# Where the summed weights of the feed-forward are kept: an SBUF tile or a PSUM bank

## The chip, the cores and the metric

The kernel runs on one core of a Trainium2 chip. Its metric is the device time of one launch in microseconds (us). A core has a matrix engine (PE, with its weight loads shown as PEld), a vector engine (DVE), a scalar engine (ACT), a general engine (POOL) and a queue engine (SP) that here issues nearly all DMAs. Each engine works through its own list of instructions in order; waits between engines are semaphores. SBUF is the on-chip working memory; PSUM, eight banks of 128 partitions by 512 fp32 values, is where PE puts its results. [...]

## The reference, cut to what matters

Two transformer layers on 512 tokens of width 1024, the first one also on 256 context tokens. Each layer ends in a gated feed-forward with 2816 hidden values, and only that part is touched:

```python
def swiglu(h, w_in, w_out):
    g, u = jnp.split(h @ w_in, 2, axis=-1)
    return (jax.nn.silu(g) * u) @ w_out
...
h = h + g2 * swiglu(modulate(h, norm2_g[l], sh2, sc2), ffn_w_in[l], ffn_w_out[l])
```

In the first layer (`l` = 0) the context tokens go through the same weights, so the feed-forward works on 768 columns there and on 512 in the second layer (`l` = 1).

## The kernel before

**The tiling.** `ffn(l)` walks over 22 inner pairs `f`. A pair is the 128 hidden values of the gate and the 128 of the up branch with the same number; its weights come in one DMA of 1024 KB, the tile `raw` of 128 x 2048 (`ffn_in`, line 792). Cut in four blocks of 128 x 512 it is `a11`, `a12` (gate, first and second half of the model width) and `a21`, `a22` (up). The tokens are cut in halves too, so the pair is a product of 2 x 2 blocks, which the kernel makes with seven block products in place of eight (Strassen's scheme in Winograd's form). The products are numbered 1 to 7 and made in the order 2, 1, 5, 6, 3, 7, 4.

**The weights of a product.** `weights(n, f, plain)` (line 915) supplies what product `n` multiplies by. Products 1, 2 and 4 take a block of `raw` as it is. Products 5, 6, 3 and 7 take a sum, made by DVE on line 925 in one tile `t` that is written anew each time:

| product | line 925 makes | tensors read |
|---|---|---|
| 5 | t = a21 + a22 | two blocks of raw |
| 6 | t = t - a11 | t and a block of raw |
| 3 | t = a12 - t | a block of raw and t |
| 7 | t = a11 - a21 | two blocks of raw |

Each block is then split into a high and a low part of the type fp32r by `slot` (line 898): ACT copies the block into the high half of a ring tile `w` (line 901), and a subtraction, block minus high part, writes the low half (line 903). That subtraction runs on DVE for the sums of pairs `f` > 2 and on POOL for everything else. The next version of `t` can be written only when the copy and the subtraction have both read the last one. The ring holds 6 slots in the first layer and 10 in the second. `mm3` multiplies the parts with three matmuls (lines 99 to 101): high by high, high by low, low by high.

**Where `t` lies.** Line 918 picks the tile once for each pair. Pairs with `f % 3 == 2` use the tile of the sums of squares (`sumsq()`, one buffer, shown as `sq` in the profile), the others use `tmp("t")`, which has two buffers. So three SBUF buffers go round by pairs. The `raw` tiles go round in the same three places, so `raw` of pair `f` + 3 is loaded when the last reader of `raw` of pair `f` is through.

**PSUM.** `fill()` (line 48) is a tag with one bank, `bank()` one with three, `wide()` one with two double banks: eight in all. In the feed-forward `fill` holds the second product of the pairs 0, 1 and 2 (line 942), and from pair 3 on product 2 goes to a `bank()`; `fill` isn't used again until the end of the feed-forward.

**The order of the work.** The pairs 0 to 2 are worked together, product by product. From pair 3 on each pair's seven products stand between parts of the second matmul of the feed-forward (`s2`, its result added into `xT` and `ctxT` on line 757). In the first layer the list is also filled up with dot products for the next layer's modulation (`junk`, line 220, DVE). The kernel's text gives priorities; a planner that simulates the engines then lays down the order of each engine's list, and an instruction is placed where the planner has its inputs and its tile ready.

DVE reads the results of the products out of PSUM: line 964 after product 1, 975 after 3, 979 after 7, 984 after 4. Products 1, 6, 7 and 4 add up in the same bank, so PE can start 4 only when line 979 has read what 7 left.

Of the kernel before, what the change touches and what calls it, by code (L numbers as in the profile page):

```python
# [26 lines left out]
class Builder:  # L27
# [814 lines left out]
    def ffn(self, l):  # L842
# [53 lines left out]
        raws, sums, state = {}, {}, {}  # L896

        def slot(src, t=None, eng=None):
            t = ring.tile([P, 2, 512], F32R, name=self.uid("w"), tag="w", bufs=(6, 10)[l]) if t is None else t
            with tc.issue_after(self.first_sq.ins) if self.nslot < 12 else ExitStack():  # L900
                nc.scalar.copy(t[:, 0, :], src)  # L901
            self.nslot += 1
            (eng or nc.gpsimd).tensor_tensor(t[:, 1, :], src, t[:, 0, :].bitcast(F32), ALU.subtract)  # L903
            return t
# [10 lines left out]
        def weights(n, f, plain):  # L915
            if f not in raws:
                raws[f] = self.raws.pop(f) if f < 2 else self.ffn_in(l, f, ring if f % 3 == 2 else self.Rf)
                sums[f] = self.sumsq()[:, :512] if f % 3 == 2 else self.tmp("t")
            r, t = raws[f], sums[f]
            a11, a12, a21, a22 = [r[:, i * 512:(i + 1) * 512] for i in range(4)]  # L920
            for v, x, y, how in ((5, a21, a22, ALU.add), (6, t, a11, ALU.subtract), (3, a12, t, ALU.subtract),
                                 (7, a11, a21, ALU.subtract)):
                if v == n:
                    with tc.issue_after(self.last_diag.ins) if both and f < 3 and n == 5 else ExitStack():
                        nc.vector.tensor_tensor(t, x, y, how)  # L925
            if plain:
                return {1: a11, 2: a12}[n]
            return slot({1: a11, 2: a12, 4: a22}[n]) if n in (1, 2, 4) else slot(t, eng=nc.vector if f > 2 else None)
# [7 lines left out]
        def product(n, f):  # L936

            plain = n in (1, 2) and f in self.plain
            w = weights(n, f, plain)
            st = state.setdefault(f, {})  # L940
            if n == 2:
# [401 lines left out]
```

## Time and profile before

| | |
|---|---|
| median of 3 runs | 1676.35 us (1673.29 to 1677.78) |
| the profiled execution | 1676.23 us, of which 1674.4 us is the span from its first to its last instruction |
| mean granted PE clock | 0.971 of full speed |
| ACT busy | 729.3 us, 44% of the span |
| POOL busy | 658.4 us, 39% |
| line 903 on POOL, low parts of plain blocks of raw | 126 x 1391 ns |
| line 901 on ACT, high parts of `t` | 120 x 621 ns |

The page gives for each engine its busy time and the number of its instructions, and then groups of instructions by source line: busy time, mean duration of one, and the idle time of the engine just before them with what ended it. A group's tile names drop their numbers, so `t` stands for every buffer of that tag. Other views give the waits between engines, the chain of work that ended last, a list of instructions in order of time, and busy times by stretch of time. The feed-forward of the first layer runs from about 410 to 960 us, that of the second from about 1255 to 1650 us.

### The profile page before, as it was taken

How to read it: one execution, taken by the hardware profiler on the slowest of the kernel's cores; microseconds unless marked ns; L12 is line 12 of the kernel's file. 1: busy time of each engine (PE TensorE's matmuls, PEld its weight loads, DVE VectorE, ACT ScalarE, POOL GpSimd, SP SyncE). 2: the span in 40 equal slices, each digit the busy share in tenths (PEclk: the TensorE clock that was granted, in tenths of full speed). 3: DMA queues.
4: the chain of work that ended last, by engine and by line, in shares of the span. 5: the costliest groups of instructions: out<-in, count | busy, mean ns of one | idle time of the engine just before them, and what ended most of it. 6: DMA issues, size and time to landing. Idle time of an engine off the chain costs nothing.

```text
span 1674.4 us, 24582 instructions
## 1 busy us (share of the span) xinstructions
PE 1550.9 (93%) x9463; PEld 1358.2 (81%) x9463; DVE 1152.9 (69%) x2097; ACT 729.3 (44%) x1464; POOL 658.4 (39%) x477
## 2 busy tenths in 40 slices
PE   6999989799889899999999988999986899999996
PEld 4776878699689899999999877767776788888886
DVE  4622788855987889777766675665668866775675
ACT  2413676533532333333333334555555444444442
POOL 0463211231563433434343236422116755545562
PEclk9999989999899999999999989999998999999998
DMA  8743000232032333444331112101140332323211
GB/s 311 298 170 145 32 7 1 76 133 82 3 123 93 134 122 121 148 139 147 130 128 38 50 60 74 51 13 43 53 158 1 127 108 81 114 76 109 82 38 51
DMA packets 47957, 161.97 MB, mean 97 GB/s; under 512 B 5472, under 2 KB 9952, under 8 KB 40160
## 3 DMA queue, kind: packets, MB, share of 16 engines
q1 hardware_dynamic: 47696, 160.28, 27.0%
q8 instruction: 74, 1.21, 0.3%
q14 instruction: 43, 0.35, 0.1%
q10 hardware_dynamic: 144, 0.13, 0.0%
HBM read 158.29 MB, written 2.10 MB: 96 GB/s over the span
## 4 chain that ended last, share of the span: by engine, by line
PE 66%; DVE 16%; DMA 6%; issue 4%; ACT 4%; POOL 4%; POOLq 0%; SPq 0%; DVEq 0%; ACTq 0%
PE pw L99 8%; PE pb L99 8%; PE pw L100 7%; PE pb L100 7%; PE pw L101 7%; PE pb L101 7%; DMA raw<-ffn_in 4%; PE pf L99 3%; PE pf L100 2%; PE pf L101 2%; PE pb L1198 2%; PE pb L1192 2%; POOL w L903 2%; DVE t L925 2%; DVE junk L220 2%
## 5 line engine op out<-in xcount | busy, mean ns | idle before, releaser
L903 POOL TENSOR_TENSOR w<-raw,w 128x512 fp32r<-128x512 f32 x126 | 173.6, 1391 | 152.2 <-ACT w L901 146.0
L99 PE MATMUL pw<-ax,w 128*128 128x384 f32 (+2 forms) x640 | 209.0, 330 | 17.2 <-DVE hs L984 5.3
L78 POOL TENSOR_TENSOR w<-raw,w 128x512 fp32r<-128x512 f32 (+1 forms) x84 | 127.1, 1520 | 235.4 <-ACT w L75 213.4
L100 PE MATMUL pw<-ax,w 128*128 128x384 f32 (+2 forms) x640 | 208.1, 325 | 2.7 <-DVE ax L456 1.4
L101 PE MATMUL pw<-ax,w 128*128 128x384 f32 (+2 forms) x640 | 206.2, 325 | 1.3 <-POOL w L903 1.1
L903 POOL TENSOR_TENSOR w<-rawo,w 128x512 fp32r<-128x512 f32 x80 | 122.2, 1527 | 198.4 <-ACT w L901 192.2
L757 DVE SCALAR_TENSOR_TENSOR xT<-pb,mod,xT 128x512 f32<-128x512 f32 (+3 forms) x208 | 144.3, 703 | 48.2 <-PE pb L101 47.8
L99 PE MATMUL pw<-T,w 128*128 128x384 f32 (+1 forms) x504 | 159.0, 318 | 17.1 <-DVE hs L975 7.4
L99 PE MATMUL pb<-hh,w 128*128 128x512 f32 x480 | 166.5, 361 | 7.4 <-ACT hh L115 5.3
L100 PE MATMUL pb<-hh,w 128*128 128x512 f32 x480 | 171.2, 358 | 0.9 <-POOL hh L116 0.9
L101 PE MATMUL pb<-hh,w 128*128 128x512 f32 x480 | 168.8, 358 | 0.5 <-POOL w L903 0.5
L100 PE MATMUL pw<-T,w 128*128 128x384 f32 (+1 forms) x504 | 159.1, 316 | 3.5 <-POOL T L116 1.8
L101 PE MATMUL pw<-T,w 128*128 128x384 f32 (+1 forms) x504 | 158.3, 314 | 0.0
L99 PEld LDWEIGHTS pw<-ax,w 128*128 128x128 f32 x640 | 122.9, 193 | 32.5 <-DVE q L979 8.3
L901 ACT CAST w<-t 128x512 fp32r<-128x512 f32 x120 | 74.4, 621 | 151.3 <-DVE t L925 111.7
L100 PEld LDWEIGHTS pw<-ax,w 128*128 128x128 f32 x640 | 123.5, 193 | 10.1 <-DVE ax L193 2.7
L101 PEld LDWEIGHTS pw<-ax,w 128*128 128x128 f32 x640 | 123.3, 193 | 6.1 <-POOL w L903 2.6
L99 PEld LDWEIGHTS pw<-T,w 128*128 128x128 f32 x504 | 97.3, 194 | 23.6 <-ACT T L115 8.8
L116 POOL TENSOR_TENSOR hh<-hs,hh 128x768 fp32r<-128x768 f32 (+1 forms) x42 | 75.9, 1809 | 85.5 <-ACT hh L115 83.1
L99 PE MATMUL pb<-ax,w 128*128 128x256 f32 (+1 forms) x340 | 105.0, 311 | 3.0 <-ACT w L75 1.6
L903 DVE TENSOR_TENSOR w<-t,w 128x512 fp32r<-128x512 f32 x104 | 89.1, 857 | 24.4 <-ACT w L901 23.4
L99 PEld LDWEIGHTS pb<-hh,w 128*128 128x128 f32 x480 | 90.1, 190 | 18.8 <-ACT hh L115 6.0
(384 smaller groups left out, 4160.2 us busy)
## 6 DMA issues: line engine op xcount, KB each, us to landing
raw<-ffn_in SPq DMA_DIRECT2D x44, 1024.0 KB, 4.9
ar<-ada SPq DMA_DIRECT2D x24, 1024.0 KB, 6.7
ar<-ada SPq DMA_DIRECT2D x48, 512.0 KB, 3.5
rawo<-ffn_out SPq DMA_DIRECT2D x44, 512.0 KB, 3.6
raw<-odd_out SPq DMA_DIRECT2D x32, 256.0 KB, 2.6
raw<-qk SPq DMA_DIRECT2D x16, 256.0 KB, 7.7
raw<-uv SPq DMA_DIRECT2D x16, 256.0 KB, 2.7
raw<-even_out SPq DMA_DIRECT2D x8, 512.0 KB, 4.4
```

The costliest lines, as they stand in the source:

```text
L78: eng.tensor_tensor(lo, raw, hi.bitcast(F32), ALU.subtract)
L99: mm(out, s[0], m[0], start=start, stop=False, **kw)
L100: mm(out, s[0], m[1], start=False, stop=False, **kw)
L101: mm(out, s[1], m[0], start=False, stop=stop, **kw)
L116: return (lo_eng or nc.vector).tensor_tensor(lo, src, hi.bitcast(F32), ALU.subtract)
L220: self.nc.vector.scalar_tensor_tensor(junk, t, 1.0, self.cb[who], ALU.mult, ALU.mult, accum_out=self.acc[who][:, col:col + 1])
L757: self.nc.vector.scalar_tensor_tensor(h, ps[:, r], self.modcol(l, j, m, who), h, ALU.mult, ALU.add)
L901: nc.scalar.copy(t[:, 0, :], src)
L903: (eng or nc.gpsimd).tensor_tensor(t[:, 1, :], src, t[:, 0, :].bitcast(F32), ALU.subtract)
L925: nc.vector.tensor_tensor(t, x, y, how)
L1192: nc.tensor.transpose(pt[:, x * P:(x + 1) * P], es[2 * (x % 2) + x // 2][:, kb * P:(kb + 1) * P], self.ident)
L1198: nc.tensor.matmul(po[64 * h:64 * h + 64, :], V[vb][:, 64 * g:64 * g + 64], t[:, h * TC:h * TC + TC], start=kb == 0, stop=kb == nb - 1, sk ...
```

## The change

From pair 3 on the tile `t` is the bank of `fill()`. Pair 2 keeps the tile of the sums of squares, and the pairs 0 and 1 keep `tmp("t")`. The additions on line 925 then write to PSUM, and for products 6 and 3 read it too; the copy on line 901 and the subtraction on line 903 read their block from PSUM. One bank takes the place of three buffers, so a pair's first sum is written into the place where the last sum of the pair before it stood.

```diff
         def weights(n, f, plain):
             if f not in raws:
                 raws[f] = self.raws.pop(f) if f < 2 else self.ffn_in(l, f, ring if f % 3 == 2 else self.Rf)
-                sums[f] = self.sumsq()[:, :512] if f % 3 == 2 else self.tmp("t")
+                sums[f] = self.fill() if f > 2 else self.sumsq()[:, :512] if f == 2 else self.tmp("t")
             r, t = raws[f], sums[f]
```

## The prediction

> **What bounds the kernel now.** I read the page's busy times first, then the busy time by stretch for the two feed-forwards from pair 3 on.
>
> ```profile
> span 1674.4 us, 24582 instructions
> PE 1550.9 (93%) x9463; PEld 1358.2 (81%) x9463; DVE 1152.9 (69%) x2097; ACT 729.3 (44%) x1464; POOL 658.4 (39%) x477
> ```
>
> ```profile
> 490.00:960.00 470.00, 462.29 (x2610) 433.19 (x2610) 352.09 (x564) 161.49 (x294) 179.03 (x117) 1.00 0.33 112
> 1310.00:1610.00 300.00, 285.17 (x1904) 259.83 (x1904) 207.13 (x306) 135.77 (x269) 156.51 (x111) 0.99 0.27 97
> ```
>
> The columns are the stretch, then busy time and count for PE, PEld, DVE, ACT and POOL, then the granted clock. PE is idle for 7.7 us of the 470 us in the first layer and for 14.8 us of the 300 us in the second. So the whole prize in these stretches is about 22 us, however much work DVE loses. The view of PE's waits says what ends this idle time, first layer, then second:
>
> ```profile
> PE pb L99 <- ACT hh L115: 5.3, 2, 3.2
> PE pb L99 <- DVE xT L757: 1.7, 3, 1.2
> PE pb L99 <- DVE ctxT L757: 0.6, 1, 0.6
> ```
>
> ```profile
> PE pw L99 <- DVE hs L984: 5.3, 6, 2.3
> PE pw L99 <- DVE q L979: 4.2, 5, 0.9
> PE pw L99 <- DVE hs L975: 1.8, 1, 1.8
> PE pw L101 <- POOL w L903: 1.1, 1, 1.1
> PE pb L100 <- POOL hh L116: 0.9, 1, 0.9
> PE pw L99 <- DVE u L979: 0.8, 1, 0.8
> PE pb L101 <- POOL w L903: 0.5, 2, 0.2
> ```
>
> The rows sum to 7.6 and 14.6 us, which is the idle time. In the second layer 12.1 us of it wait for DVE, though DVE is busy only 207 of 300 us. The chain of work that ended last shows why (start, length, what):
>
> ```profile
> 1410.38 6.90 DMA raw<-ffn_in
> ...
> 1417.34 0.57 issue
> 1417.91 0.68 DVE w L903
> 1418.59 0.34 DVE hs L984
> ...
> 1418.98 0.39 PE pw L99
> ```
>
> A load of `raw` lands, and only then does DVE go on to a subtraction, to line 984, and so to PE. DVE's list and its waits (second row group) complete this:
>
> ```profile
> 1352.91 0.69 DVE L925 TENSOR_TENSOR t<-raw 128x512 f32<-128x512 f32 x1 [3.23 <-DMA raw<-ffn_in]
> 1406.52 0.69 DVE L903 TENSOR_TENSOR w<-sq,w 128x512 fp32r<-128x512 f32 x1 [0.74 <-ACT w L901]
> 1417.30 0.69 DVE L925 TENSOR_TENSOR sq<-raw 128x512 f32<-128x512 f32 x1 [2.28 <-DMA raw<-ffn_in]
> 1450.32 0.68 DVE L903 TENSOR_TENSOR w<-sq,w 128x512 fp32r<-128x512 f32 x1
> ```
>
> ```profile
> DVE w L903 <- ACT w L901: 16.0, 27, 0.8
> DVE t L925 <- DMA raw<-ffn_in: 13.7, 6, 3.2
> DVE sq L925 <- DMA raw<-ffn_in: 6.2, 2, 3.9
> ```
>
> At 1417.30 DVE makes the first sum (product 5) of a pair whose `raw` has just landed, after standing 2.28 us for it. Its tile `sq` had been free since 1406.52 (the last subtraction of the pair before it in that tile), and the sum's own subtraction comes at 1450.32, 33 us later. Three buffers let the planner put this sum two pairs early, at the head of an in-order list, and line 984 waits behind it. This head-of-line stall costs DVE 19.9 us in the stretch (13.7 + 6.2). **That, and not DVE's load, is the larger part of PE's waiting.**
>
> **The change part by part.** It adds and removes no instruction. It alters what 152 subtractions, 152 copies and 152 sums touch (19 pairs x 4 sums x 2 layers), and when a pair's first sum may run.
>
> *1. DVE durations.* Groups with shapes kept apart, over the run (busy, mean ns, idle before):
>
> ```profile
> L903 DVE TENSOR_TENSOR w<-t,w 128x512 fp32r<-128x512 f32 x104 | 89.1, 857 | 24.4 <-ACT w L901 23.4
> L903 DVE TENSOR_TENSOR w<-sq,w 128x512 fp32r<-128x512 f32 x48 | 42.3, 881 | 8.4 <-ACT w L901 7.9
> L925 DVE TENSOR_TENSOR t<-raw,t 128x512 f32<-128x512 f32 x30 | 35.8, 1193 | 1.2 <-POOL w L903 0.8
> L925 DVE TENSOR_TENSOR t<-t,raw 128x512 f32<-128x512 f32 x30 | 27.6, 919 | 0.2
> L925 DVE TENSOR_TENSOR sq<-raw,sq 128x512 f32<-128x512 f32 x14 | 13.1, 936 | 0.2
> L925 DVE TENSOR_TENSOR sq<-sq,raw 128x512 f32<-128x512 f32 x14 | 11.8, 844 | 0.2
> ```
>
> The nearest rows with one operand in PSUM are the same subtraction in the attention, and line 757, which runs all through the feed-forward beside POOL (min/median/max):
>
> ```profile
> L116 DVE TENSOR_TENSOR atl<-pb,ath 128x512 fp32r<-128x512 f32 x28 | 19.1, 683 | 3.1 <-ACT ath L115 3.1
> ```
>
> ```profile
> L757 DVE SCALAR_TENSOR_TENSOR xT<-pb,mod,xT x208: 337/740/752, 375.5 to 1658.8; 128x512 f32<-128x512 f32 x88, 128x256 f32<-128x256 f32 x12, 128x384 f32<-128x384 f32 x2, 128x128 f32<-128x128 f32 x2
> L757 DVE SCALAR_TENSOR_TENSOR ctxT<-pb,mod,ctxT x98: 466/474/488, 400.4 to 964.9; 128x256 f32<-128x256 f32 x98
> ```
>
> Line 757 never exceeds 752 ns, while operations with both inputs in SBUF average 844 to 1193 ns. I read that as DVE losing time to POOL only where it reads two SBUF tensors. At 683 ns the 152 subtractions go from 131.4 to 103.8 us, saving 27.6. Product 6's sums average (27.6 + 11.8)/44 = 0.895 us, so 38 of them save 8.1; product 3's average (35.8 + 13.1)/44 = 1.111 us, so 38 save 16.3. Together DVE loses about 52 us of busy time. The sums for 5 and 7 still read two SBUF blocks and keep their length. Most of this lies beside a busy PE and is worth nothing there: PE is busy 98% in the first layer.
>
> [...]
>
> No row shows DVE writing to PSUM, or reading and writing one bank in one instruction. From below: such writes might gain what ACT gains by PSUM, some 0.03 us each (rows in part 2). From above: one more pass over the elements. Line 757 takes 740 ns for 512 and 474 for 256 elements, 1.04 ns each, so up to 0.53 us for each of 152 sums, 81 us of DVE. I take zero, by the 683 ns row, and keep 81 for the range: in the 300 us of the second layer 18 pairs x 4 x 0.53 = 38 us would bring DVE from 207 to 245 us at most, 82%, before any saving.
>
> *2. ACT.*
>
> ```profile
> L901 ACT CAST w<-t 128x512 fp32r<-128x512 f32 x120 | 74.4, 621 | 151.3 <-DVE t L925 111.7 <-PE pb L101 17.3 <-PE pw L101 16.0
> L115 ACT CAST ath<-pb 128x512 fp32r<-128x512 f32 x28 | 16.5, 589 | 7.2 <-PE pb L554 7.1
> ```
>
> Reading PSUM, the copy falls from 621 to 589 ns, 4.9 us over 152. ACT is busy under half of these stretches; this counts as nothing.
>
> *3. The early sums.* With one bank, pair f+1's first sum must follow the last subtraction of pair f. Its `raw` landed about a pair earlier, so DVE no longer stands for the load. All of the 5.3 us on line 984 (six waits, on the pattern of the chain above) and the 1.8 us on line 975, which follows the 3.23 us stall at 1352.91, should go: **7.1 us**. What is late next is product 4 behind line 979, whose 5.0 us stay.
>
> *4. The clock.* After the two longest of these waits PE was granted little more than half its clock for 4 us:
>
> ```profile
> 1356.00:1360.00 4.00, 4.00 (x17) 3.47 (x16) 2.79 (x6) 1.16 (x3) 0.26 (x1) 0.57 0.00 0
> 1520.00:1524.00 4.00, 4.00 (x20) 3.71 (x19) 3.19 (x3) 1.75 (x5) 2.97 (x2) 0.57 0.00 0
> ```
>
> That is 2 x 4 x 0.43 = **3.4 us** more, which goes with its cause.
>
> *5. The first layer's start.* The only place where DVE's load itself holds PE:
>
> ```profile
> 536.00:626.00 90.00, 82.92 (x469) 78.07 (x468) 80.39 (x124) 30.61 (x56) 33.10 (x21) 1.00 0.35 123
> ```
>
> DVE is busy 80.4 of 90 us, and both waits for `hh` (5.3 us) lie here. Shorter subtractions help, but the `junk` dot products behind them also read two SBUF tensors and will meet POOL instead. I count half, **2.6 us**.
>
> *6. The added wait.* The pair's first sum, 0.69 us, now stands in front of its copy and subtraction, and DVE may wait 0.74 us for that copy, as in the row at 1406.52. Behind it in DVE's list are lines 757, 964, 975, 979 and 984, for which ACT and PE wait. The weights themselves are some ten slots early in the second layer, six in the first, so this hits only what is queued behind. I charge **1.1 us**, 0.2 for each of the six waits on line 979.
>
> Sum: 7.1 + 3.4 + 2.6 - 1.1 = 12.0 us. From the profiled execution, 1676.23, that gives **1664**; the median of 1676.35 is the same within 0.1.
>
> **The rivals.**
>
> *More than that.* The planner lays the list out anew, and a lighter DVE answers at once everywhere: all 22.2 us of waits and the 3.4 of clock go, 1651. For it: 5.0 us of the rest wait for DVE. Against: line 979 lies directly between products 7 and 4, and POOL's 2.5 us stay.
>
> *The waits only move.* The DMA stall leaves DVE, but the sums, now on demand, put DVE behind ACT instead (16.0 us of such waits exist already), or the subtraction still loses time to POOL because its other input is in SBUF. Then the gain of part 3 is given back: 1675. Against the latter: the attention's subtraction has the same operands and takes 683.
>
> *Slower: the single bank's chain.* Each pair gets 0.69 + 0.74 = 1.43 us of sum and wait in DVE's list. If it lands ahead of line 979 or 984 just when PE waits for it, in each of some 17 pairs of the second layer, that is 24.3 us against 10.5 gained there: 1690. It breaks even at about 7 pairs. For it: PE waits for DVE in that place already, five times 0.8 us. Against: the planner placed such sums away from it so far, and DVE has 93 idle us in that stretch.
>
> **How the numbers follow.** Forecast 1664, chance 0.50. More than that, 1651, 0.13. The waits only move, 1675, 0.23. Slower, 1690, 0.14. What this measurement can tell from no change is about 0.3%, 5 us. So faster 0.63, same 0.23, slower 0.14. The range runs from 1651 to 1682: dear PSUM sums (up to 8 us in the first layer's start, where some 15 of them run) and half of the slower case are in it; the rest of that case and a little below 1651 are left out.
>
> **What would show it.** [...] Step 3: no DVE wait of line 925 for `raw`, and no PE wait on line 984. Step 4: no 4 us at 0.57 after 1340. Step 5: waits for `hh` near 2.6 us. Step 6: DVE's waits for line 901 above 16.0 us, and line 979's waits above 5.0. The prediction is wrong if PE's waits on DVE keep their sum under other names, or if the planner's new order opens idle time elsewhere.

## The result, and the profile after

| | before | after |
|---|---|---|
| median | 1677.07 us (4 runs, 1673.29 to 1679.1) | 1650.9 us (4 runs, 1648.77 to 1652.44) |
| ratio, 95% interval | | 0.9844 (0.9825 to 0.9863) |
| span of the profiled execution | 1674.4 us | 1650.6 us |

The change takes 26 us off, more than twice the 12 us forecast, and the median lies 0.1 us below the range. The page after, first lines:

```profile
span 1650.6 us, 24613 instructions
PE 1542.3 (93%) x9463; PEld 1357.8 (82%) x9463; DVE 1111.1 (67%) x2097; ACT 725.6 (44%) x1464; POOL 651.4 (39%) x477
```

DVE loses 41.8 us, PE 8.6 us, though PE runs the same 9463 matmuls. To see where the span shrank, compare both feed-forwards. In the first layer the additions into `ctxT` on line 757 start at 400.4 and 964.9 us (first and last, a row quoted in the prediction), and after:

```profile
L757 DVE SCALAR_TENSOR_TENSOR ctxT<-pb,mod,ctxT x98: 468/477/487, 403.8 to 964.0; 128x256 f32<-128x256 f32 x98
```

That is 564.5 against 560.2 us: 4.3 us. The 3.4 us by which the later kernel starts there are lost ahead of anything the change touches. The second layer gives the rest. Busy time by stretch, before and then after, from the last product of the first three pairs to the last line 984 (columns as in the prediction):

```profile
1315.30:1647.50 332.20, 314.39 (x2089) 285.52 (x2088) 225.34 (x332) 145.41 (x290) 171.92 (x121) 0.99 0.24 84
```

```profile
1315.30:1623.70 308.40, 306.49 (x2089) 283.28 (x2089) 204.46 (x332) 142.47 (x290) 164.69 (x121) 1.00 0.26 91
```

The same 2089 matmuls take 23.8 us less: 15.9 us less idle time (17.8 to 1.9) and 7.9 us less busy time. PE's waits in this stretch summed to 17.5 us in 21 waits; after, three are left:

```profile
PE pw L99 <- ACT u L972: 0.7, 1, 0.7
PE pw L99 <- DVE hs L975: 0.6, 1, 0.6
PE pw L99 <- DVE q L979: 0.5, 1, 0.5
```

The groups that answer to those on lines 903 and 925 (now `pf`, the bank) have these minimum, median and maximum durations:

```profile
L925 DVE TENSOR_TENSOR pf<-raw x76: 684/699/2329, 480.0 to 1602.8; 128x512 f32<-128x512 f32 x76
L925 DVE TENSOR_TENSOR pf<-pf,raw x38: 681/689/690, 485.0 to 1596.2; 128x512 f32<-128x512 f32 x38
L925 DVE TENSOR_TENSOR pf<-raw,pf x38: 677/685/686, 487.1 to 1598.5; 128x512 f32<-128x512 f32 x38
```

```profile
L903 DVE TENSOR_TENSOR w<-pf,w x152: 673/686/694, 484.4 to 1605.5; 128x512 fp32r<-128x512 f32 x152
```

Each of these 228 operations with one input in PSUM stays under 0.7 us, reading and writing one bank included; 104 of them run beside a POOL instruction, and they take 676 to 693 ns. The sums for 5 and 7, whose two inputs lie in SBUF, still reach 2.3 us. DVE's waits in the second layer, 1310 to 1610 us, begin thus, and none is on a load:

```profile
DVE w L903 <- ACT w L901: 26.7, 27, 2.6
DVE xT L757 <- PE pb L101: 16.7, 18, 1.9
DVE q L979 <- PE pw L101: 15.7, 6, 3.1
```

### The profile page after: what moved, and what is told of

It reads as the page before. It is cut to its first block, busy times and chain, and to the rows that moved or that the text cites. A ratio compares the mean times of both kernels' runs of the same rounds, so it can differ in the third digit from the quotient of the medians.

```text
span 1650.6 us, 24613 instructions
## 1 busy us (share of the span) xinstructions
PE 1542.3 (93%) x9463; PEld 1357.8 (82%) x9463; DVE 1111.1 (67%) x2097; ACT 725.6 (44%) x1464; POOL 651.4 (39%) x477
## 4 chain that ended last, share of the span: by engine, by line
PE 81%; DVE 11%; ACT 3%; issue 2%; POOL 1%; DMA 1%; POOLq 0%; SPq 0%; DVEq 0%; ACTq 0%
PE pw L99 10%; PE pw L100 10%; PE pw L101 10%; PE pb L100 10%; PE pb L101 10%; PE pb L99 10%; PE pf L99 3%; PE pf L100 2%; PE pf L101 2%; PE pb L1198 2%; PE pb L1192 2%; PE pf L349 2%; PE pw L1156 1%; DVE t L925 1%; PE pw L1164 1%
## 5 line engine op out<-in xcount | busy, mean ns | idle before, releaser
L903 POOL TENSOR_TENSOR w<-raw,w 128x512 fp32r<-128x512 f32 x126 | 184.1, 1468 | 143.3 <-ACT w L901 134.3
L903 POOL TENSOR_TENSOR w<-rawo,w 128x512 fp32r<-128x512 f32 x80 | 114.1, 1427 | 215.2 <-ACT w L901 206.1
L901 ACT CAST w<-pf 128x512 fp32r<-128x512 f32 x152 | 89.4, 588 | 181.5 <-DVE pf L925 59.8
L903 DVE TENSOR_TENSOR w<-pf,w 128x512 fp32r<-128x512 f32 x152 | 104.3, 686 | 41.6 <-ACT w L901 38.4
L99 PE MATMUL pb<-ax,w 128*128 128x256 f32 (+1 forms) x340 | 105.1, 311 | 3.3 <-ACT w L75 1.6
L100 PE MATMUL pb<-ax,w 128*128 128x256 f32 (+1 forms) x340 | 104.7, 308 | 0.9 <-DVE ax L116 0.9
L901 ACT CAST w<-raw 128x512 fp32r<-128x512 f32 x126 | 76.6, 622 | 64.4 <-PE pw L101 62.5
```

Source lines behind the costliest of these rows:

```text
L99: mm(out, s[0], m[0], start=start, stop=False, **kw)
L100: mm(out, s[0], m[1], start=False, stop=False, **kw)
```

## The experiments

Two theories stood after the result. A: the gain is that a first sum is no longer made two pairs early, so DVE doesn't stand for its load. B: the gain is that an operation with a PSUM operand doesn't lose time to POOL. The change does both at once.

**One SBUF tile: A without B.** The order of the change, the place of before.

```diff
-                sums[f] = self.sumsq()[:, :512] if f % 3 == 2 else self.tmp("t")
+                sums[f] = self.sumsq()[:, :512] if f > 1 else self.tmp("t")
```

> One SBUF tile (the tile of the sums of squares) for the summed weights from pair 3 on: the same single-buffer order as the change, without PSUM. Theory A (the gain is DVE no longer standing for the load of a sum made two pairs early): 1650 to 1657 us, no DVE wait of line 925 for raw in the second layer, two pairs of the second layer every 31.3 us as in the changed kernel, although the subtractions on line 903 still average over 0.8 us. Theory B (the gain is that operations with one PSUM operand do not lose time to POOL): 1670 us or more, two pairs every 32.5 us or more.

Measured: 1663.65 us against 1679.89, ratio 0.991 (0.9888 to 0.9931), 16 us less. Neither theory: it lies between, and so does the pace, two pairs every 31.8 us (some 33.2 before, 31.3 after the change). DVE's waits for `raw` and PE's on line 984 are gone, while the subtractions average 908 ns. Of the waits on line 979, 5.0 us before, 1.8 are left (1310 to 1610 us):

```profile
PE pw L99 <- DVE q L979: 1.3, 5, 0.3
...
PE pw L99 <- DVE u L979: 0.5, 2, 0.3
```

**The first sum early, the others in PSUM: B without A.**

```diff
             r, t = raws[f], sums[f]
+            s = t
+            if f > 2 and n in (6, 3, 7):
+                if n == 6:
+                    later[f] = self.fill()
+                t = later[f]
...
-            for v, x, y, how in ((5, a21, a22, ALU.add), (6, t, a11, ALU.subtract), (3, a12, t, ALU.subtract),
+            for v, x, y, how in ((5, a21, a22, ALU.add), (6, s, a11, ALU.subtract), (3, a12, t, ALU.subtract),
```

> The sum for product 5 stays in three SBUF tiles and may run two pairs early; only the sums for 6, 3 and 7 lie in the PSUM bank, so three quarters of the subtractions and the sums for 6 and 3 are without POOL's interference (the sum for 6 reads two SBUF tiles again). Theory A: the early sum still stands for its load, about 20 us of DVE waits on line 925 in the second layer, PE waits on line 984 stay, 1668 to 1677 us. Theory B: three quarters of the gain, 1655 to 1661 us.

Measured: 1665.23 us, ratio 0.9921 (0.9902 to 0.994), 15 us less; again between. Its list of DVE (five lines further down: 930 is 925, 989 is 984) and PE's longest wait in the second layer:

```profile
1411.91 0.69 DVE L930 TENSOR_TENSOR sq<-raw 128x512 f32<-128x512 f32 x1 [2.58 <-DMA raw<-ffn_in]
1412.52 0.68 DVE L903 TENSOR_TENSOR w<-t,w 128x512 fp32r<-128x512 f32 x1
1413.12 0.42 DVE L989 TENSOR_TENSOR hs<-hs,pw 128x256 f32<-128x256 f32 x1
```

```profile
PE pw L99 <- DVE hs L989: 6.9, 7, 1.7
```

The early sum still stands for its load and line 984 still waits behind it: PE waits on it for 8.3 us in all (a second row has 1.4), against 5.3 before. But no PE wait on line 979 is left in the stretch. So B alone takes away the waits on 979 and none of those on 984, and A alone takes away those on 984 and 3.2 of the 5.0 us on 979. The halves alone give 16 and 15 us, where the change gives 26. That would be an overlap of some 5 us, but the intervals of the three ratios are 3 to 4 us wide to each side, and this run is no clean half: a quarter of its subtractions and the sums for product 6 still read two SBUF tiles, and its waits on 984 grew. The overlap is not shown.

**Each layer alone.** The bank in the second layer, then in the first (`l == 0`); elsewhere the tiles of before.

```diff
-                sums[f] = self.sumsq()[:, :512] if f % 3 == 2 else self.tmp("t")
+                sums[f] = self.fill() if f > 2 and l == 1 else self.sumsq()[:, :512] if f % 3 == 2 else self.tmp("t")
```

> The change in the second layer alone. By the two traces, where the second feed-forward became 23 us shorter and the first 4: 1652 to 1657 us under both theories. If the gain needed the first layer's tiles as well: over 1660.

> The change in the first layer alone. Both theories: 1671 to 1675 us, about 4 us under before, since PE is idle for under 8 us there. Theory B more than A: DVE is busy 80 of 90 us at this layer's start, so what is gained should lie between 530 and 630 us. If nothing: 1675 to 1679.

Measured: 1657.89 us, ratio 0.9872 (0.985 to 0.9894), 22 us less, and 1674.09 us, ratio 0.9971 (0.9961 to 0.9981), 6 us less. The second layer carries four fifths, and the two add up within their noise (28 us against 26). The first time is 1 us over its range; the second is as expected, but only about half of the first layer's gain lies between 530 and 630 us, going by the start times of the same matmuls in the two traces. The rest builds up slowly until the layer's end.

**Two SBUF tiles.** A first sum may run one pair ahead.

```diff
-                sums[f] = self.sumsq()[:, :512] if f % 3 == 2 else self.tmp("t")
+                sums[f] = self.sumsq()[:, :512] if f == 2 else self.tmp("t")
```

> Two SBUF tiles in turn for the summed weights, so a first sum may be made one pair early, not two. If what hurts is a first sum made as early as its load lands (three tiles, as many as there are tiles of raw): as good as one SBUF tile, 1660 to 1667 us, no DVE wait of line 925 for raw. If any sum made ahead of its pair hurts: 1668 us or more.

Measured: 1662.58 us against 1678.8, ratio 0.99 (0.9885 to 0.9915), as with one. DVE waits for a load on line 925 for 1.0 us in the whole run. So what hurt is what the third tile allows: with as many as there are tiles of `raw`, a sum can be placed where its load only just lands.

**Three tiles, the first sum held back.** All tiles as before, but each pair's first sum is issued only after the last sum of the pair before.

```diff
-                    with tc.issue_after(self.last_diag.ins) if both and f < 3 and n == 5 else ExitStack():
-                        nc.vector.tensor_tensor(t, x, y, how)
+                    held = n == 5 and f > 3
+                    with (tc.issue_after(self.last_diag.ins) if both and f < 3 and n == 5 else
+                          tc.issue_after(self.last_sum.ins) if held else ExitStack()):
+                        ins = nc.vector.tensor_tensor(t, x, y, how)
+                    if n == 7:
+                        self.last_sum = ins
```

> The kernel before with its three SBUF tiles, but each pair's first sum may be issued only after the last sum of the pair before it. If the early first sum is what costs, and not the number of tiles: as one SBUF tile, 1660 to 1668 us, no DVE wait of line 925 for raw in the second layer. If the tiles matter in another way (their release, the loads): 1674 us or more.

Measured: 1669.92 us against 1678.64, ratio 0.9949 (0.993 to 0.9967), 9 us less; 2 us over the range for A. The DVE waits for loads and the PE waits on line 984 are gone, as A says, and those on line 979 fall to 1.1 us. But the planner's list is another one, and it has a wait that none of the other kernels above has at that size (1310 to 1610 us; at most 0.5):

```profile
PE pb L99 <- DVE xT L757: 6.1, 7, 1.2
```

So this run supports A's mechanism and not its size.

**The planner's share.** The planner knows where a tile lies, so a PSUM tile also changes its lists. Three kernels do without its simulation: before, one SBUF tile, and the change.

```diff
-    with tile.TileContext(nc, schedule_with_timeline_sim=True) as tc:
+    with tile.TileContext(nc, schedule_with_timeline_sim=False) as tc:
```

One SBUF tile and the bank then get nearly the same lists: in the first layer they differ by one swap on DVE, two on ACT and two moved matmuls, in the second by a few swaps of neighbours in each pair.

> The kernel before with its lists laid down without the planner's simulation. No forecast of its time; it is the base for the next two, whose lists then differ little.

> One SBUF tile, lists without the planner's simulation. With np_after it tells the chip's share (PSUM operands) from the planner's: the two have the same lists in the first layer but for a few places.

> The change, lists without the planner's simulation. If PSUM operands themselves shorten the time (no conflict with POOL on DVE): at least 6 us under np_one_sbuf, with fewer and shorter PE waits on DVE, since one SBUF tile is 12.8 us over the change with the planner. If the rest of the gain was a better list from the planner: within 3 us of np_one_sbuf.

Measured: 1785.34, 1744.31 and 1720.51 us. All are slower than before (1678.8), since the lists are worse. One tile in place of three is worth 41 us here (line 925 waited 66 us for loads), and the bank in place of that tile another 24. The groups of the two, shapes apart (busy, mean ns, idle before):

```profile
L903 DVE TENSOR_TENSOR w<-sq,w 128x512 fp32r<-128x512 f32 x152 | 125.3, 824 | 50.2 <-ACT w L901 48.5 <-PE pb L101 0.7
```

```profile
L903 DVE TENSOR_TENSOR w<-pf,w 128x512 fp32r<-128x512 f32 x152 | 104.5, 687 | 46.4 <-ACT w L901 45.5
```

PE's waits on lines 975, 979 and 984 over the run fall from 17.4 to 5.2 us. In the first layer, where the lists are all but the same, the additions into `ctxT` run from 421.8 to 996.0 us with one SBUF tile and from 419.4 to 986.8 with the bank, 6.8 us less. PSUM operands therefore shorten the time on the chip itself. Their size is that of these lists; how the gain of the lists by simulation divides between the operands and a better order stays open.

**Who lengthens the operations.** POOL writes zeros in place of its subtractions on line 903 (the low parts of the plain blocks are left out), all else as before:

```diff
-            (eng or nc.gpsimd).tensor_tensor(t[:, 1, :], src, t[:, 0, :].bitcast(F32), ALU.subtract)
+            if eng is None:
+                nc.gpsimd.memset(t[:, 1, :].bitcast(F32), 0.0)
+            else:
+                eng.tensor_tensor(t[:, 1, :], src, t[:, 0, :].bitcast(F32), ALU.subtract)
```

> The kernel before, with POOL writing zeros in place of its subtractions on line 903 (the low parts of the plain weight blocks are left out of the computation): POOL then writes the same tiles in the same places of its list and reads no SBUF there. If DVE's subtractions and sums on lines 903 and 925 are long because POOL reads SBUF beside them: their mean falls from 0.86 and 0.95 us to under 0.76, in SBUF tiles all the same. If they are long for another reason (SBUF as such, semaphores): unchanged over 0.83. The time is not compared, since POOL's list also gets shorter.

```profile
L906 DVE TENSOR_TENSOR w<-t,w 128x512 fp32r<-128x512 f32 x104 | 79.9, 768 | 21.8 <-ACT w L901 20.9
L906 DVE TENSOR_TENSOR w<-sq,w 128x512 fp32r<-128x512 f32 x48 | 36.2, 754 | 10.0 <-ACT w L901 9.5
```

The subtractions (here line 906) average (79.9 + 36.2)/152 = 0.764 us against 0.864 before, with SBUF tiles: just over the 0.76 expected. Over the 0.686 of the changed kernel, 56% of the excess is gone. The sums for 6 and 3 go from 1.00 to 0.74 us. What is left comes from POOL's subtractions on line 116, which still read SBUF. The traces show this operation by operation, for DVE's 328 operations on lines 903 and 925. Before, 167 have no POOL instruction beside them and take 670 to 694 ns; the 107 that take over 750 all lie beside a POOL subtraction. With the zeros, 67 lie beside nothing of POOL's but such a write and take 674 to 694 ns, and all 27 that take over 750 lie beside line 116. So DVE's operations are long beside POOL's subtractions, which read SBUF, and not beside its writes of zeros. The time, 1611.62 us, is no measure of it, since POOL's writes of zeros are also shorter than its subtractions on this line (526 ns on average against 1448).

## Why the prediction failed where it did

**Part 1, the durations, held; what it made of them did not.** It gave 683 ns and the chip shows 686, with no price for a PSUM source or a bank read and written at once; the three savings come to 50 us of DVE where it had 52. Its sums for 5 and 7 did not keep their length: from 0.88 to 0.97 us on average, they take 8 us back. But it added that most of the saving "is worth nothing" beside a busy PE. The three operations ahead of line 979 show otherwise. Before, with POOL's list under DVE's:

```profile
1420.27 1.23 DVE L903 TENSOR_TENSOR w<-t,w 128x512 fp32r<-128x512 f32 x1 [0.41 <-ACT w L901]
1421.53 1.66 DVE L925 TENSOR_TENSOR t<-raw,t 128x512 f32<-128x512 f32 x1
1423.96 0.69 DVE L903 TENSOR_TENSOR w<-t,w 128x512 fp32r<-128x512 f32 x1 [0.76 <-ACT w L901]
1424.57 0.41 DVE L979 TENSOR_TENSOR u<-u,pw 128x256 f32<-128x256 f32 x1
```

```profile
1419.65 1.30 POOL L116 TENSOR_TENSOR hh<-hs,hh 128x512 fp32r<-128x512 f32 x1 [3.48 <-ACT hh L115]
1420.91 1.74 POOL L903 TENSOR_TENSOR w<-rawo,w 128x512 fp32r<-128x512 f32 x1
```

DVE's subtraction at 1420.27 ends 0.55 us after POOL's at 1419.65 does, the sum at 1421.53 ends 0.54 us after POOL's next: both last until some 0.55 us after POOL's instruction has ended, as if they could do most of their work only then (an undisturbed one takes 0.69). From the first to line 979 it is 4.30 us, and PE waits 0.84. With one SBUF tile the same stretch takes 4.30 us too, but lies earlier against PE, which waits 0.27. After:

```profile
1409.26 0.69 DVE L903 TENSOR_TENSOR w<-pf,w 128x512 fp32r<-128x512 f32 x1
1409.86 0.69 DVE L925 TENSOR_TENSOR pf<-raw,pf 128x512 f32<-128x512 f32 x1
1411.27 0.69 DVE L903 TENSOR_TENSOR w<-pf,w 128x512 fp32r<-128x512 f32 x1 [0.73 <-ACT w L901]
1411.88 0.41 DVE L979 TENSOR_TENSOR u<-u,pw 128x256 f32<-128x256 f32 x1
```

2.62 us, and no wait.

The two long rows take 0.5 and 1.0 us more than the undisturbed 0.69. The whole trace of before agrees: all 107 operations on lines 903 and 925 that take over 750 ns end 545 to 559 ns after a POOL subtraction has ended. With one PSUM input the mean after the change is 686 ns; with two SBUF inputs and no POOL instruction beside them it was 685 before. No price for the PSUM source shows.

**Part 3 is the step that failed.** Its first half held: no DVE wait for `raw`, no PE wait on line 984, and the stall on 975 gone. Its second half, that product 4 behind line 979 is late next and its "5.0 us stay", is wrong. From 1310 to 1610 us none of the 5.0 is left, with one SBUF tile 1.8, in the early-sum run none. Over the longer stretch above these waits fell from 6.6 to 0.5 us, and POOL's 2.5 us went too. Both halves of the change did it: the new order, which alone moves DVE's work away from the moment when PE needs line 979, and the shorter operations, which take the rest.

**Part 4 held, and lacked a term.** The two stretches at 0.57 of the clock are gone: from 1340 to 1640 us the granted clock is 1.00 after. But busy time fell by 7.9 us, not 3.4. The other 4.5 us, over 18 waits less, are 0.25 us a wait. PE's list before shows where:

```profile
1418.07 0.28 PE L101 MATMUL pw<-ax,w 128*128 128x256 f32 x1
1418.98 0.39 PE L99 MATMUL pw<-ax,w 128*128 128x256 f32 x1 [0.63 <-DVE hs L984]
1419.20 0.28 PE L100 MATMUL pw<-ax,w 128*128 128x256 f32 x1
1419.32 0.28 PE L101 MATMUL pw<-ax,w 128*128 128x256 f32 x1
```

Matmuls of this shape start 0.12 us apart; here one starts after 0.91 and the next after 0.22, so the halt costs 0.89 us where the row of waits has 0.63. All the waits look so: by the start times in PE's list the 21 of before cost 5.5 us beyond their rows, the three of after 0.8. That is 4.8 us of restarts less, 0.26 a wait, about the 4.5 left over. With one SBUF tile as many matmuls, 2089 (1318.9 to 1635.5 us) have 14 waits and 309.84 us busy, 3.35 over the changed kernel for 11 waits more: 0.30 each. The prediction put this term at nothing.

**Part 5** forecast 2.6 us for the first layer, and 4.3 came (with the change there alone 4.5, 401.4 to 961.4 us in the row of `ctxT`), but not by the step that it names. The waits for `hh` did not halve. From 490 to 960 us after:

```profile
PE pb L99 <- ACT hh L115: 3.8, 3, 2.7
PE pb L100 <- POOL hh L116: 1.9, 2, 1.3
```

That is 5.7 us against 5.3. What went are the 2.3 us behind line 757; the rest shows in no row of PE's waits, and its cause stays open. One SBUF tile gives 0.5 (403.5 to 967.5), and without the simulation the bank was worth 6.8 us here over one SBUF tile; both point to B.

**Part 6** charged 1.1 us that were not paid. DVE's waits for the copies did rise, from 16.0 to 26.7 us, but they fell where PE does not wait.

So the second layer's sum of 9.4 us (7.1 + 3.4 - 1.1) should have been 15.7 of waits, 3.4 of clock and 4.8 of restarts: 23.9, against 23.8 measured. The first rival, 1651, had the time right, in part by luck: it let all waits go, and 5.7 of the first layer's 7.6 us stayed, but the restarts that it did not count filled their place. The range stopped at it because its sum knew no restarts either. The slower rival's price is refuted: the single bank's chain put no new wait on PE.

## What to carry to other kernels

A tile that lets an in-order engine take work early can cost more than it saves: here one or two tiles fewer than there are places for loads kept DVE from standing for a load at the head of its list (19.9 us of such waits from 1310 to 1610 us before, none there with one tile, 1.0 us in the whole run with two), and either took 16 us off. When DVE shares its time with POOL, count the SBUF tensors that each operation reads; a free PSUM bank for one of them made the subtraction's duration steady here, 673 to 694 ns where it had been 671 to 2318. And price a wait of PE by more than its row, since each one here cost about 0.26 us beyond it.

## What the runs showed of the hardware

In the changed kernel a DVE sum that reads and writes the same PSUM bank took 677 to 690 ns for 512 values, as long as an operation between SBUF tiles took before with no POOL instruction beside it (670 to 694); the prediction had left room for 0.53 us more. ACT's copy of the high part took 588 ns from the bank against 621 from SBUF. And POOL writing zeros, with no tensor read, held up no DVE operation that reads two SBUF tensors: the 67 that ran beside such writes alone took 674 to 694 ns, and all 27 over 750 ns lay beside POOL's subtractions on line 116.
